# First feed-forward product in Strassen's form: 7 block products of 384 columns per pair of strips in place of 8

## The chip, the core and the metric

The kernel runs on one core of one Trainium2 chip. The metric is the device time of one execution in microseconds; beside each timed run stands one profiled execution with its trace. TensorE (PE in the profile) does the matmuls and loads their weights (PEld); VectorE (DVE), ScalarE (ACT) and GpSimd (POOL) do the element-wise work; SyncE (SP) issues most transfers.

## The reference

Two layers are applied to 768 tokens: 512 of a prompt and 256 of a sample. Only the second line of a layer is changed:

```
x = x + W_o( g_att * P_att(DiffAttn(n)) + g_rec * P_rec(BiRGLRU(n)) ),  n = RMSNorm(x)
h2 = rmsnorm(x, norm2_g)
x = x + jnp.square(jax.nn.relu(h2 @ w_ff1)) @ w_ff2      # 1024 -> 4096 -> 1024
```

## The kernel before

Everything is kept transposed: channels on the 128 partitions, the 768 tokens along the free axis, in two groups g of 512 and 256 (`GROUPS`). A float32 value is held as a rounded part hi and a remainder lo. Each product is three matmuls into one PSUM bank: hi by hi, hi by lo, lo by hi (`mm3`, L251 to L253). `split` makes the two parts: hi by a copy on ACT (L197), lo by a subtraction on DVE (L200).

**Weights.** A transfer of 512 KB brings 128 x 1024 numbers into one of two buffers `raw`; they are split into `whi` and `wlo`, four buffers each (`prefetch`, L233). A plan lists the strips in the order of use, and preparation may run 8 strips ahead.

**End of the mixers.** `wo_part` (L867) adds the 8 strips of `W_o` to the residual `xt`. `prep` (L294, L295) multiplies `xt` by the gain of the norm and splits it into `n2h` and `n2l`. The norm's factor over the tokens, `rb`, is not applied there but to the hidden values after the first product. For it, `squares` squares the 8 tiles of a group on ACT (L307), sums them on DVE in a chain of 7 dependent additions (L311) and splits the sum into two tiles `s`. `stats` sums `s` over the partitions by two matmuls with ones per group (L335, L336; result `nps`), and ACT and DVE make `rb` of it (L283 to L288).

**Feed-forward part.** 8 chunks c of 512 hidden channels per layer. In each, the first product FF1 has 4 strips s by 2 groups by 8 tiles of the contraction by 3 matmuls: 192, of 512 or 256 columns. Each result becomes hidden values: DVE takes the positive part times `rb` (L909), ACT squares it (L910), and it is split into `hh` and `hl`. The second product FF2 has 192 matmuls too, over the 4 tiles of the chunk, and its results are added to `xt` (L924). After the last chunk of layer 1 they go to the output (L929). In the chunk c = 0 the statistics stand on PE behind the first two strips, which are 96 matmuls, and their hidden values wait for `rb`.

**Order.** PE's order is the order of the program text. On the other engines a scheduler sorts the instructions when the kernel is built; each engine then works through its list in order.

Of the kernel before, what the change touches and what calls it, by code (L numbers as in the profile page):

```python
# [72 lines left out]
def trunk_kernel(ctx: ExitStack, tc: tile.TileContext, xT, wqk, wv, wx, wy, wg0, wg1, wa, wr, wo, wf1, wf2,  # L73
# [32 lines left out]
    def small_params(l, ap_):  # L106
# [99 lines left out]
    for l in range(DEPTH):  # L206
# [172 lines left out]
    for l in range(DEPTH):  # L379
# [453 lines left out]
        for j in range(KT):  # L833
            if j >= NF:
                w1 = wload("wr", l, j)
            m = ep.tile([P, T], F32, tag="sg", name=nm("m"), bufs=2)
# [8 lines left out]
            if j < 4:  # L845
                hi = recp.tile([P, T], F32R, tag="r", name=nm("mh"))
                lo = recp.tile([P, T], F32R, tag="r", name=nm("ml"))
            else:
                hi, lo = slot(gl, F32R), slot(gl, F32R)
# [10 lines left out]
        wso = {}  # L860

        def wo_part(j, g):
            if j not in wso:
                wso[j] = wload("wo", l, j)
            off, n = GROUPS[g]
            ps = strip(ppf, wso[j], (mh, ml), g)
            V.tensor_tensor(out=xt[j][:, off:off + n], in0=xt[j][:, off:off + n], in1=ps, op=ALU.add)  # L867

        LAG = 0
        for j in range(KT + LAG):  # L870
            if j < KT:
                wo_part(j, 0)
            if j >= LAG:
                wo_part(j - LAG, 1)


        n2h = [ep.tile([P, T], F32R, tag="e", name=nm("n2h")) for k in range(KT)]
# [7 lines left out]
        for c in range(NC_):  # L885
# [129 lines left out]
```

## Time and profile before

| | us |
|---|---|
| median of 3 runs (lowest, highest) | 2740.41 (2739.55, 2741.24) |
| the profiled execution | 2740.3 |
| its span | 2738.5 |
| PE busy | 2706.5 (99%) |
| DVE busy | 1639.8 (60%) |
| ACT busy | 1321.9 (48%) |

The feed-forward part of layer 0 runs from 838.9 to about 1373 us of the span, that of layer 1 from about 2201 to 2735. Matmuls overlap in the pipeline, so their durations add up to more than the time; what one costs is read from the distance between two starts.

### The profile page before, as it was taken

How to read it: one execution, taken by the hardware profiler on the slowest of the kernel's cores; microseconds unless marked ns; L12 is line 12 of the kernel's file. 1: busy time of each engine (PE TensorE's matmuls, PEld its weight loads, DVE VectorE, ACT ScalarE, POOL GpSimd, SP SyncE). 2: the span in 40 equal slices, each digit the busy share in tenths (PEclk: the TensorE clock that was granted, in tenths of full speed). 3: DMA queues.
4: the chain of work that ended last, by engine and by line, in shares of the span. 5: the costliest groups of instructions: out<-in, count | busy, mean ns of one | idle time of the engine just before them, and what ended most of it. 6: DMA issues, size and time to landing. Idle time of an engine off the chain costs nothing.

```text
span 2738.5 us, 41111 instructions
## 1 busy us (share of the span) xinstructions
PE 2706.5 (99%) x16840; PEld 2437.8 (89%) x16840; DVE 1639.8 (60%) x2970; ACT 1321.9 (48%) x2293; POOL 96.1 (4%) x134
## 2 busy tenths in 40 slices
PE   8999999999999999999999999999999999999999
PEld 8999888888888888888899998888888888888888
DVE  8878873797545443444578878637984454444443
ACT  7777871568324222222367878616773242222221
POOL 0000000000110000000000000000002100000000
PEclk9999999999999999999999999999999999999999
DMA  3111123121321112111221111231223211121111
GB/s 130 58 44 62 42 101 109 55 70 66 132 92 62 62 64 68 62 62 62 99 74 45 57 47 51 97 108 53 72 70 139 85 62 62 62 69 63 62 62 70
DMA packets 57485, 199.36 MB, mean 73 GB/s; under 512 B 7504, under 2 KB 9936, under 8 KB 57296
## 3 DMA queue, kind: packets, MB, share of 16 engines
q1 hardware_dynamic: 48384, 161.50, 17.8%
q0 software_dynamic: 8192, 34.61, 3.5%
q8 instruction: 132, 2.16, 0.3%
q10 hardware_dynamic: 720, 0.62, 0.1%
q14 instruction: 57, 0.47, 0.1%
HBM read 177.83 MB, written 18.87 MB: 72 GB/s over the span
## 4 chain that ended last, share of the span: by engine, by line
PE 86%; DVE 7%; ACT 5%; issue 1%; DMA 0%; ACTq 0%; DVEq 0%
PE d L251 19%; PE d L252 19%; PE d L253 19%; PE d L399 4%; PE d L398 4%; PE d L397 4%; PE s L574 3%; PE d L276 2%; PE d L275 2%; PE d L277 2%; PE d L526 1%; PE d L524 1%; PE d L525 1%; DVE t L808 1%; PE t L597 1%
## 5 line engine op out<-in xcount | busy, mean ns | idle before, releaser
L197 ACT ACTIVATE whi<-raw 128x1024 fp32r<-128x1024 f32 (+1 forms) x304 | 315.0, 1037 | 771.1 <-PE d L252 627.7
L200 DVE TENSOR_TENSOR wlo<-raw,whi 128x1024 fp32r<-128x1024 f32 (+1 forms) x304 | 369.5, 1217 | 120.5 <-ACT whi L197 119.0
L252 PE MATMUL d<-n2l,whi 128*128 128x512 f32 (+1 forms) x1024 | 344.8, 337 | 0.0
L251 PE MATMUL d<-n2h,whi 128*128 128x512 f32 (+1 forms) x1024 | 344.5, 336 | 0.0
L253 PE MATMUL d<-n2h,wlo 128*128 128x512 f32 (+1 forms) x1024 | 344.1, 336 | 0.0
L252 PE MATMUL d<-sX,whi 128*128 128x512 f32 (+1 forms) x704 | 237.0, 337 | 0.0
L251 PE MATMUL d<-sY,whi 128*128 128x512 f32 (+1 forms) x640 | 215.4, 337 | 0.3 <-DVE rec L344 0.3
L253 PE MATMUL d<-sY,wlo 128*128 128x512 f32 (+1 forms) x640 | 215.1, 336 | 0.0
L251 PEld LDWEIGHTS d<-n2h,whi 128*128 128x128 f32 x1024 | 194.4, 190 | 20.8
L253 PEld LDWEIGHTS d<-n2h,wlo 128*128 128x128 f32 x1024 | 194.2, 190 | 20.5
L252 PEld LDWEIGHTS d<-n2l,whi 128*128 128x128 f32 x1024 | 194.4, 190 | 20.0
L910 ACT ACTIVATE fr<-fr 128x512 f32<-128x512 f32 (+1 forms) x128 | 65.9, 515 | 270.6 <-DVE fr L909 270.6
L909 DVE SCALAR_TENSOR_TENSOR fr<-d,rb 128x512 f32<-128x512 f32 (+1 forms) x128 | 71.4, 558 | 176.5 <-PE d L253 168.9
L252 PE MATMUL d<-hl,whi 128*128 128x256 f32 (+1 forms) x512 | 172.4, 337 | 0.0
L251 PE MATMUL d<-hh,whi 128*128 128x256 f32 (+1 forms) x512 | 172.3, 336 | 0.0
L253 PE MATMUL d<-hh,wlo 128*128 128x256 f32 (+1 forms) x512 | 172.0, 336 | 0.0
L924 DVE TENSOR_TENSOR sZ<-sZ,d 128x256 f32<-128x256 f32 (+1 forms) x128 | 71.0, 554 | 141.6 <-PE d L253 141.6
L251 PE MATMUL d<-sZ,whi 128*128 128x512 f32 (+1 forms) x448 | 150.8, 337 | 0.3 <-DVE rec L344 0.3
L252 PE MATMUL d<-sZ,whi 128*128 128x512 f32 (+1 forms) x448 | 150.8, 336 | 0.0
L253 PE MATMUL d<-sZ,wlo 128*128 128x512 f32 (+1 forms) x448 | 150.6, 336 | 0.0
L397 PE MATMUL d<-whi,sY 128*128 128x256 f32 x512 | 147.8, 289 | 0.0
L397 PE MATMUL d<-whi,sZ 128*128 128x256 f32 x512 | 147.8, 289 | 0.0
(311 smaller groups left out, 7373.0 us busy)
## 6 DMA issues: line engine op xcount, KB each, us to landing
raw<-wf SPq DMA_DIRECT2D x128, 512.0 KB, 3.2
raw<-wqk SPq DMA_DIRECT2D x32, 512.0 KB, 3.3
raw<-wg SPq DMA_DIRECT2D x32, 512.0 KB, 3.3
raw<-wv SPq DMA_DIRECT2D x16, 512.0 KB, 3.8
raw<-wa SPq DMA_DIRECT2D x16, 512.0 KB, 4.2
raw<-wx SPq DMA_DIRECT2D x16, 512.0 KB, 3.3
raw<-wy SPq DMA_DIRECT2D x16, 512.0 KB, 3.2
raw<-wr SPq DMA_DIRECT2D x16, 512.0 KB, 3.4
```

What stands on the lines that cost most here:

```text
L197: S.activation(hi, src, AF.Copy)
L200: V.tensor_tensor(out=lo, in0=src, in1=hi.bitcast(F32), op=ALU.subtract)
L251: PE.matmul(ps, lhsT=wh, rhs=xh, start=(k == 0), stop=False)
L252: PE.matmul(ps, lhsT=wh, rhs=xl, start=False, stop=False)
L253: PE.matmul(ps, lhsT=wl, rhs=xh, start=False, stop=(k == n - 1))
L397: PE.matmul(j, lhsT=xh, rhs=hi[:, kk], start=(k == 0), stop=False)
L398: PE.matmul(j, lhsT=xh, rhs=lo[:, kk], start=False, stop=False)
L399: PE.matmul(j, lhsT=xl, rhs=hi[:, kk], start=False, stop=(k == 7))
L574: PE.matmul(pss[c], lhsT=z["q"][:, c, qs], rhs=kk[:, c, off:off + n], start=(x == 0), stop=(x == 1))
L909: V.scalar_tensor_tensor(out=r_, in0=ps, scalar=0.0, in1=rb2[:, off:off + n], op0=ALU.max, op1=ALU.mult)
L910: S.activation(r_, r_, AF.Square, scale=0.5)
L924: V.tensor_tensor(out=xg, in0=xg, in1=ps, op=ALU.add)
```

## The change

The tokens are cut into two halves of 384 (`TS`), the contraction of FF1 into two halves of 4 tiles, and the strips of a chunk into two pairs p. For each pair the 2 x 2 x 2 = 8 block products become 7 (`FP` lists all 14 of a chunk as p and product number), each of 4 tiles by 3 matmuls of 384 columns. That is 168 matmuls per chunk in place of 192.

**Operands of the tokens.** The 7 operands are scaled values or sums of blocks of `xt`, with the gain applied and split: products 1 and 5 from `ff_prep1` while the first four strips of `W_o` run, 6, 7 and 4 from `ff_prep2` in the next four, 2 and 3 behind them. They replace `prep`.

**Operands of the weights.** Four transfers bring a1, b1, b2, a2 (a1 and b1 into two new buffers `rw`); four DVE additions of 128 x 1024 make P1, P2, P3 and P4 of them, and the 7 operands a1, P1, P2, a2, P3, b2, P4 are each split. So a chunk has 11 splits of weights in place of 8, with the 4 of FF2.

**Results.** A PSUM bank takes several products where Strassen's form only adds them; otherwise ACT copies the bank out (L987, L989, L994) and DVE adds or subtracts (L991, L995, L1000): 6 copies and 6 additions per chunk. `hidden` is called 8 times per chunk, on 384 columns. FF2 keeps 192 matmuls, now all of 384 columns, with 16 additions to `xt` (L1015).

**Statistics.** In the chunk c = 0 they stand behind 6 of the 14 products, which are 72 matmuls.

```diff
...
+TH = T // 2
+TS = (slice(0, TH), slice(TH, T))
...
+FW = ("a1", "P1", "P2", "a2", "P3", "b2", "P4")
+FP = ((0, 1), (1, 1), (0, 5), (1, 5), (0, 6), (1, 6), (0, 2), (0, 7), (1, 2), (1, 7), (0, 4), (0, 3), (1, 4), (1, 3))
...
-            plan += [("wf1", l, c * 4 + s) for s in range(4)] + [("wf2", l, c * 4 + s) for s in range(4)]
+            plan += [("wf1", l, c, x) for x in FW] + [("wf2", l, c * 4 + s) for s in range(4)]
     pos = [0]
+    fw, fpool = {}, [None]
+    def ff_operand(l, c, x):
+        ep_ = fpool[0]
+        if x == "a1":
+            for i, y in enumerate(("a1", "b1", "b2", "a2")):
+                if i < 2:
+                    fw[y] = ep_.tile([P, 1024], F32, tag="rw", name=nm("rw"), bufs=2)
+                else:
+                    fw[y] = wp.tile([P, 1024], F32, tag="raw", name=nm("raw"), bufs=2)
+                nc.sync.dma_start(out=fw[y], in_=wf1[l][c][i])
+        elif x in ("P1", "P2"):
+            u, v = ("b1", "b2") if x == "P1" else ("P1", "a1")
+            fw[x] = ep_.tile([P, 1024], F32, tag="ws", name=nm("ws"), bufs=2)
+            V.tensor_tensor(out=fw[x], in0=fw[u], in1=fw[v], op=ALU.add)
+        elif x == "P3":
+            fw[x] = fw["b1"]
+            V.tensor_tensor(out=fw[x], in0=fw["a1"], in1=fw["b1"], op=ALU.add)
+        elif x == "P4":
+            fw[x] = fw["P2"]
+            V.tensor_tensor(out=fw[x], in0=fw["P2"], in1=fw["a2"], op=ALU.add)
+        return fw[x]
...
+        def halves(o, k):
+            ops[o][k] = t_ = slot(gx, F32R) if o in (1, 5) else rslot(F32R) if o in (2, 3) else eslot(F32R)
+            return t_[:, 0:TH], t_[:, TH:T]
+        def split2(o, k, src, gain=None):
+            hi, lo = halves(o, k)
+            if gain is None:
+                split(hi, lo, src)
+            else:
+                S.activation(hi, src, AF.Copy, scale=gain)
+                V.scalar_tensor_tensor(out=lo, in0=src, scalar=gain, in1=hi.bitcast(F32), op0=ALU.mult, op1=ALU.subtract)
+        gn = lambda k: v_[:, V_N2 + k:V_N2 + k + 1]
+        diff = [eslot() for i in range(2)]
+        def ff_prep1(k):
+            x, d = xt[k], diff[k // 2][:, TS[k % 2]]
+            split2(1, k, x[:, TS[0]], prm["ng2"][:, k:k + 1])
+            V.tensor_tensor(out=d, in0=x[:, TS[0]], in1=x[:, TS[1]], op=ALU.subtract)
+            split2(5, k, d, gn(k))
+        def ff_prep2(k):
+            x, x2, d = xt[k], xt[k + 4], diff[k // 2][:, TS[k % 2]]
+            t_ = eslot()
+            u, w = (t_[:, t] for t in TS)
+            S.activation(u, x2[:, TS[1]], AF.Copy, scale=gn(k + 4))
+            V.scalar_tensor_tensor(out=w, in0=d, scalar=gn(k), in1=u, op0=ALU.mult, op1=ALU.add)
+            split2(6, k, w)
+            V.scalar_tensor_tensor(out=u, in0=x[:, TS[1]], scalar=gn(k), in1=u, op0=ALU.mult, op1=ALU.subtract)
+            split2(7, k, u)
+            V.scalar_tensor_tensor(out=w, in0=x2[:, TS[0]], scalar=gn(k + 4), in1=w, op0=ALU.mult, op1=ALU.subtract)
+            split2(4, k, w)
+        for j in range(KT):
+            w1 = wload("wo", l, j)
+            for g in range(2):
+                off, n = GROUPS[g]
+                ps = strip(ppf, w1, (mh, ml), g)
+                V.tensor_tensor(out=xt[j][:, off:off + n], in0=xt[j][:, off:off + n], in1=ps, op=ALU.add)
+            if j < 4:
+                ff_prep1(j)
+            else:
+                ff_prep2(j - 4)
+        for o in (2, 3):
+            for k in range(4):
+                split2(o, k, xt[k + 4][:, TS[o - 2]], gn(k + 4))
...
+            def hidden(s, t, z, r_):
+                for i in range(2):
+                    if (s, i) not in hs:
+                        hs[s, i] = slot(gl, F32R) if not last else eslot(F32R) if s < 2 else rslot(F32R)
+                hi, lo = (hs[s, i][:, TS[t]] for i in range(2))
+                V.scalar_tensor_tensor(out=r_, in0=z, scalar=0.0, in1=rb2[:, TS[t]], op0=ALU.max, op1=ALU.mult)
+                S.activation(r_, r_, AF.Square, scale=0.5)
+                split(hi, lo, r_)
...
+            for i, (p, q) in enumerate(FP):
+                x, b = {1: ("a1", 2), 5: ("P1", 3), 6: ("P2", 2), 2: ("a2", 1), 7: ("P3", 2), 4: ("b2", 2), 3: ("P4", 3)}[q]
+                if x not in ws:
+                    ws[x] = [a.rearrange("p (h k c) -> p h k c", h=2, c=P)[:, :] for a in wload("wf1", l, c, x)]
+                hi, lo = (a[:, p] for a in ws[x])
+                new = q in (1, 5, 2)
+                if new:
+                    bank[p, b] = ppf.tile([P, TH], F32, tag="d", name=nm("d"))
+                ps = bank[p, b]
+                for k in range(4):
+                    oh, ol = (ops[q][k][:, t] for t in TS)
+                    PE.matmul(ps, lhsT=hi[:, k], rhs=oh, start=new and k == 0, stop=False, skip_group_check=True)
+                    PE.matmul(ps, lhsT=hi[:, k], rhs=ol, start=False, stop=False, skip_group_check=True)
+                    PE.matmul(ps, lhsT=lo[:, k], rhs=oh, start=False, stop=k == 3, skip_group_check=True)
+                m1, m16, u3, y4 = (z[:, TS[p]] for z in zz)
+                if q == 1:
+                    S.activation(m1, ps, AF.Copy, scale=-1.0)
+                elif q == 6:
+                    S.activation(m16, ps, AF.Copy, scale=-1.0)
+                elif q == 2:
+                    V.tensor_tensor(out=m1, in0=m1, in1=ps, op=ALU.add)
+                    hidden(2 * p, 0, m1, m1)
+                elif q == 7:
+                    S.activation(u3, ps, AF.Copy)
+                    V.tensor_tensor(out=u3, in0=u3, in1=bank[p, 3], op=ALU.subtract)
+                    hidden(2 * p + 1, 1, u3, u3)
+                elif q == 4:
+                    hidden(2 * p + 1, 0, ps, y4)
+                elif q == 3:
+                    V.tensor_tensor(out=m16, in0=m16, in1=ps, op=ALU.add)
+                    hidden(2 * p, 1, m16, m16)
+                if c == 0 and i == 5:
                     for g_ in range(2):
                         stats(nss[g_], rb2, None, g_, lambda n, s: mp.tile([P, n], F32, tag=gl, name=nm(s)), ppf, "d")
...
+            for s in range(4):
+                hi, lo = (a.rearrange("p (j k c) -> p j k c", j=2, c=P) for a in wload("wf2", l, c * 4 + s))
+                for t in range(2):
+                    for jj in range(2):
+                        j = 2 * s + jj
+                        ps = ppf.tile([P, TH], F32, tag="d", name=nm("d"))
+                        mm3(ps, [(hi[:, jj, k], lo[:, jj, k], hs[k, 0][:, TS[t]], hs[k, 1][:, TS[t]])
+                                 for k in ((0, 1, 2, 3), (0, 1, 3, 2))[t]])
+                        xg = xt[j][:, TS[t]]
+                        V.tensor_tensor(out=xg, in0=xg, in1=ps, op=ALU.add)
...
```

On PE, at the statistics of layer 0 (`nps` the sums; `s` the split sums of squares, first of 512 tokens, then of 256), before:

```order
L253 MATMUL d_1642_9398<-n2h_1595_9207,wlo_1555_8797 128x256
L335 MATMUL nps_1643_9423<-s_1613_9272,ones_71 128x512
L336 MATMUL nps_1643_9423<-s_1614_9273,ones_71 128x512
L335 MATMUL nps_1646_9434<-s_1623_9299,ones_71 128x256
L336 MATMUL nps_1646_9434<-s_1624_9300,ones_71 128x256
L251 MATMUL d_1656_9470<-n2h_1588_9200,whi_1559_8854 128x512
```

and now (lines of the changed kernel; `e`, `r` are operands of the tokens):

```order
L984 MATMUL d_1650_9391<-e_1610_9277,wlo_1569_8879 128x384
L370 MATMUL nps_1659_9469<-s_1630_9336,ones_71 128x512
L371 MATMUL nps_1659_9469<-s_1631_9337,ones_71 128x512
L370 MATMUL nps_1662_9480<-s_1640_9363,ones_71 128x256
L371 MATMUL nps_1662_9480<-s_1641_9364,ones_71 128x256
L982 MATMUL d_1671_9502<-r_1613_9288,whi_1574_8941 128x384
```

The statistics still stand in one block, now behind the sixth product. On DVE, where the sums of squares `sq` are made in layer 0, before:

```order
L867 TENSOR_TENSOR sY_1547_8734<-sY_1547_8734,d_1587_9174 128x256
L311 TENSOR_TENSOR sq_1605_9249<-sq_1605_9249,sq_1607_9254 128x512
L200 TENSOR_TENSOR wlo_1565_8913<-raw_1563_8910,whi_1564_8912 128x1024
L295 SCALAR_TENSOR_TENSOR n2l_1603_9215<-sY_1547_8734,vec0_78,n2h_1595_9207 128x256
L311 TENSOR_TENSOR sq_1605_9249<-sq_1605_9249,sq_1608_9257 128x512
...
L200 TENSOR_TENSOR s_1614_9273<-sq_1605_9249,s_1613_9272 128x512
...
L200 TENSOR_TENSOR wlo_1570_8971<-raw_1568_8968,whi_1569_8970 128x1024
...
L200 TENSOR_TENSOR s_1624_9300<-sq_1615_9276,s_1623_9299 128x256
L200 TENSOR_TENSOR wlo_1575_9029<-raw_1573_9026,whi_1574_9028 128x1024
```

and now, from the last addition of `W_o` (L941) on:

```order
L941 TENSOR_TENSOR sY_1547_8736<-sY_1547_8736,d_1608_9248 128x256
...
L209 TENSOR_TENSOR wlo_1581_9006<-rw_1551_8742,whi_1580_9005 128x1024
...
L346 TENSOR_TENSOR sq_1622_9313<-sq_1622_9313,sq_1623_9315 128x512
L346 TENSOR_TENSOR sq_1622_9313<-sq_1622_9313,sq_1624_9318 128x512
L209 TENSOR_TENSOR wlo_1589_9076<-raw_1552_8744,whi_1588_9075 128x1024
L346 TENSOR_TENSOR sq_1622_9313<-sq_1622_9313,sq_1625_9321 128x512
...
L209 TENSOR_TENSOR s_1631_9337<-sq_1622_9313,s_1630_9336 128x512
L209 TENSOR_TENSOR wlo_1597_9147<-ws_1567_8876,whi_1596_9146 128x1024
L346 TENSOR_TENSOR sq_1632_9340<-sq_1632_9340,sq_1633_9342 128x256
...
L209 TENSOR_TENSOR s_1641_9364<-sq_1632_9340,s_1640_9363 128x256
```

Before, one of the 7 additions of the first group (L311) stands ahead of the last addition of `W_o`. Now all 14 stand behind it, and behind 13 other instructions first: 11 of 384 columns and two splits of weights. The split of b2 (`wlo_1589`) stands between the second and the third addition, that of P4 (`wlo_1597`) ahead of the whole second group. The order in layer 1 is the same. On DVE, at the join of FF1 and FF2 in the third chunk of layer 0, before:

```order
L909 SCALAR_TENSOR_TENSOR fr_1730_10111<-d_1729_10086,rb_1604_9216 128x256
L200 TENSOR_TENSOR wlo_1690_9785<-raw_1688_9782,whi_1689_9784 128x1024
L200 TENSOR_TENSOR hl_1702_9851<-fr_1730_10111,hh_1701_9850 128x256
L924 TENSOR_TENSOR sY_1540_8720<-sY_1540_8720,d_1734_10122 128x512
L924 TENSOR_TENSOR sY_1541_8722<-sY_1541_8722,d_1735_10136 128x512
```

and now (`sZ` holds the hidden values; `rw` and `raw` are b1 and b2 of the next chunk, `ws` its P1):

```order
L209 TENSOR_TENSOR sZ_1815_10623<-e_1783_10431,sZ_1814_10622 128x384
L1000 TENSOR_TENSOR e_1781_10429<-e_1781_10429,d_1793_10485 128x384
L209 TENSOR_TENSOR wlo_1796_10501<-raw_1794_10498,whi_1795_10500 128x1024
L964 SCALAR_TENSOR_TENSOR e_1781_10429<-e_1781_10429,rb_1621_9312 128x384
L1015 TENSOR_TENSOR sY_1540_8722<-sY_1540_8722,d_1823_10709 128x384
L248 TENSOR_TENSOR ws_1806_10562<-rw_1798_10532,raw_1799_10534 128x1024
L209 TENSOR_TENSOR sZ_1813_10603<-e_1781_10429,sZ_1812_10602 128x384
```

Ahead of the last remainder of the hidden values there now stands an addition for the next chunk's weights, which needs the transfer of that chunk's b2.

## Rows read from the trace of the kernel before

**Rows 1.** The page: busy time by engine, and the chain by engine

```profile
PE 2706.5 (99%) x16840; PEld 2437.8 (89%) x16840; DVE 1639.8 (60%) x2970; ACT 1321.9 (48%) x2293; POOL 96.1 (4%) x134
...
PE 86%; DVE 7%; ACT 5%; issue 1%; DMA 0%; ACTq 0%; DVEq 0%
```

**Rows 2.** Waits of PE: line, waited for: us in total, times, longest us

```profile
PE t L546 <- DVE q L554: 8.2, 10, 1.8
PE d L475 <- ACT sY L294: 7.3, 1, 7.3
```

**Rows 3.** Windows, a chunk each: length; busy us by engine; clock, DMA share, GB/s

```profile
839.00:906.00 67.00, 67.00 (x387) 59.24 (x386) 37.76 (x61) 26.25 (x48) 0.00 (x0) 1.00 0.19 63
...
1039.00:1106.00 67.00, 67.00 (x388) 59.34 (x388) 27.25 (x40) 16.45 (x24) 0.00 (x0) 1.00 0.19 63
```

**Rows 4.** Timeline of PE in FF2 and at its end: start us, us, instruction

```profile
1099.77 0.39 PE L252 MATMUL d<-hl,whi 128*128 128x512 f32 x1
...
1103.39 0.39 PE L253 MATMUL d<-hh,wlo 128*128 128x512 f32 x1
1103.62 0.28 PE L251 MATMUL d<-hh,whi 128*128 128x256 f32 x1
...
1106.49 0.40 PE L251 MATMUL d<-n2h,whi 128*128 128x512 f32 x1
```

**Rows 5.** Timeline of PE around the statistics of layer 0

```profile
838.91 0.40 PE L251 MATMUL d<-n2h,whi 128*128 128x512 f32 x1
...
855.59 0.39 PE L335 MATMUL nps<-s,ones 128*128 128x512 f32 x1
...
856.29 0.39 PE L251 MATMUL d<-n2h,whi 128*128 128x512 f32 x1
```

**Rows 6.** Timeline of DVE there (x5: five in a row)

```profile
842.17 3.87 DVE L311 TENSOR_TENSOR sq<-sq,sq 128x512 f32<-128x512 f32 x5
846.74 0.69 DVE L200 TENSOR_TENSOR s<-sq,s 128x512 fp32r<-128x512 f32 x1 [0.70 <-ACT s L197]
...
848.92 1.23 DVE L200 TENSOR_TENSOR wlo<-raw,whi 128x1024 fp32r<-128x1024 f32 x1
850.06 2.01 DVE L311 TENSOR_TENSOR sq<-sq,sq 128x256 f32<-128x256 f32 x4
852.55 0.42 DVE L200 TENSOR_TENSOR s<-sq,s 128x256 fp32r<-128x256 f32 x1 [0.48 <-ACT s L197]
```

**Rows 7.** Timeline of ACT there

```profile
846.07 0.63 ACT L197 ACTIVATE s<-sq 128x512 fp32r<-128x512 f32 x1 [2.53 <-DVE sq L311]
...
847.84 1.05 ACT L197 ACTIVATE whi<-raw 128x1024 fp32r<-128x1024 f32 x1
848.79 1.32 ACT L307 ACTIVATE sq<-sY 128x256 f32<-128x256 f32 x4
```

**Rows 8.** Groups on DVE by form, 1039 to 1106: busy us, mean ns, idle

```profile
L200 DVE TENSOR_TENSOR wlo<-raw,whi 128x1024 fp32r<-128x1024 f32 x8 | 9.8, 1226 | 4.4 <-ACT whi L197 4.4
L924 DVE TENSOR_TENSOR sY<-sY,d 128x512 f32<-128x512 f32 x8 | 5.5, 687 | 10.0 <-PE d L253 10.0
L924 DVE TENSOR_TENSOR sY<-sY,d 128x256 f32<-128x256 f32 x8 | 3.4, 421 | 7.1 <-PE d L253 7.1
```

**Rows 9.** Groups on ACT by form, 1039 to 1106

```profile
L910 ACT ACTIVATE fr<-fr 128x512 f32<-128x512 f32 x4 | 2.5, 632 | 18.7 <-DVE fr L909 18.7
```

**Rows 10.** Timeline of PE at the start of the span

```profile
9.80 0.42 PE L475 MATMUL d<-whi,sY 128*128 128x256 f32 x1
...
12.57 0.39 PE L476 MATMUL d<-wlo,sY 128*128 128x256 f32 x1
12.79 0.30 PE L477 MATMUL d<-whi,sZ 128*128 128x256 f32 x1
```

**Rows 11.** Transfers from 906 to 972: KB each, median us from issue to landing

```profile
raw<-wf SPq DMA_DIRECT2D x8, 512.0 KB, 3.3
```

**Rows 12.** Timeline of DVE at the end of the span

```profile
2735.28 0.42 DVE L924 TENSOR_TENSOR sZ<-sZ,d 128x256 f32<-128x256 f32 x1 [1.02 <-PE d L253]
```

More of the change, by code (lines that the diff above doesn't have):

```diff
@@ L844, in trunk_kernel @@
             G.tensor_tensor(out=m, in0=m, in1=sg, op=ALU.add)
[L845 to L849, printed above, removed]
+            hi, lo = (rslot(F32R) if j < 4 else slot(gl, F32R) for i in range(2))
             split(hi, lo, m)
@@ L859, in trunk_kernel @@
             xt.append(t_)
[L860 to L874, printed above, removed]
@@ L877, in trunk_kernel @@
[L877 to L878 removed]
+        ops = {o: [None] * 4 for o in range(1, 8)}
+        def halves(o, k):
[8 more added lines that the diff above has]
+                V.scalar_tensor_tensor(out=lo, in0=src, scalar=gain, in1=hi.bitcast(F32), op0=ALU.mult, op1=ALU.subtract)
@@ L885, in trunk_kernel @@
         for c in range(NC_):
-            hh, hl, ws = [], [], {}
-            for s in range(4):
-                if c % 2 == 1:
-                    hh.append(recp.tile([P, T], F32R, tag="r", name=nm("hh")))
-                    hl.append(recp.tile([P, T], F32R, tag="r", name=nm("hl")))
-                else:
-                    hh.append(slot(gx, F32R))
-                    hl.append(slot(gx, F32R))
-            order = [(s, g) for s in range(4) for g in range(2)]
-            wait = []
-            for s, g in order:
-                if s not in ws:
-                    ws[s] = wload("wf1", l, c * 4 + s)
-                wait.append((s, g, strip(ppf, ws[s], (n2h, n2l), g)))
-                if c == 0 and s < 2:
-                    if (s, g) != (1, 1):
-                        continue
+            last = c == NC_ - 1
@@ new lines, in trunk_kernel @@
+            ws, bank = {}, {}
+            zz = [eslot() for i in range(4)]
+            for i, (p, q) in enumerate(FP):
[30 more added lines that the diff above has]
+                if c == 0 and i == 5:
@@ L904, in trunk_kernel @@
                     for g_ in range(2):
                         stats(nss[g_], rb2, None, g_, lambda n, s: mp.tile([P, n], F32, tag=gl, name=nm(s)), ppf, "d")
-                for s_, g_, ps in wait:
-                    off, n = GROUPS[g_]
-                    r_ = ep.tile([P, n], F32, tag="sg", name=nm("fr"), bufs=2)
-                    V.scalar_tensor_tensor(out=r_, in0=ps, scalar=0.0, in1=rb2[:, off:off + n], op0=ALU.max, op1=ALU.mult)
-                    S.activation(r_, r_, AF.Square, scale=0.5)
-                    split(hh[s_][:, off:off + n], hl[s_][:, off:off + n], r_)
@@ L912, in trunk_kernel @@
[L912 to L929 removed]
+            for s in range(4):
[8 more added lines that the diff above has]
+                        V.tensor_tensor(out=xg, in0=xg, in1=ps, op=ALU.add)
+                        if last:
+                            if l + 1 < DEPTH:
+                                G.dma_start(out=xs[j][:, TS[t]], in_=xg)
+                            else:
+                                nc.sync.dma_start(out=out[j][:, TS[t]], in_=xg)
```

57 lines of the change are left out of this document (23 added, 34 removed).

## The prediction

> **What bounds the kernel now.** I read the page first. PE is busy for 2706.5 of 2738.5 us, and 86% of the chain of work that ended last is PE's [rows 1]. The waits of PE come next: the largest single one is 7.3 us at the start of the span, the largest sum 8.2 us in ten pieces in attention, and none is named in the feed-forward part [rows 2]. In the windows of one chunk each PE is busy for all of 67 us at a clock of 1.00, DVE for 37.76 us in the chunk with the statistics and 27.25 us in an ordinary one, ACT for 26.25 and 16.45 [rows 3]. So this part lasts as long as its matmuls, and a matmul less is time gained, unless another engine takes that away. For what one matmul takes I read the timeline, from start to start: 16 steps from 1099.77 to 1103.39 give 0.226 us for 512 columns, 24 steps from 1103.62 to 1106.49 give 0.120 us for 256 [rows 4].
>
> **What is gained.** No matmul of 384 columns stands in the feed-forward part of before. The two sizes bound it, 0.120 and 0.226; I take the middle, 0.173 us, since a cost that grows evenly with the columns lies there. A product of 12 matmuls takes 2.08 us. FF1 of a chunk was 96 x (0.226 + 0.120) = 33.2 us and becomes 168 x 0.173 = 29.1; FF2 keeps its columns: 192 x 0.173 = 33.2. The gain is 24 x 0.173 = 4.15 us per chunk, 66.4 us in 16 chunks. At the ends of the bound the 360 matmuls would take 43 or 81 us in place of the 66.4 of before, 370 us gained or 240 lost in 16 chunks; a cost that stays at either end over a change of 128 columns is unlikely, and rival 4 keeps it.
>
> The row says 0.226 and 0.120. The Trainium skill (TensorE: Matmul & The Clock Gate, "Back-to-back issue gap") gives the columns over 2.4 GHz plus about 2.5 ns, which is 0.216, 0.109 and, at 384, 0.1625 us. Both sizes in the trace are 10 ns longer, so the trace disagrees with the rule by a constant, and the row decides; by the rule the gain would be 62.4 us.
>
> **What is added and hidden.** Costs at 384 columns are taken half way between the rows of 512 and 256: 0.55 us on DVE (0.687 and 0.421) [rows 8], about 0.5 on ACT (0.632 at 512) [rows 9]. When such instructions stand in a row the next starts some 0.08 earlier (848.92 to 850.06 is 1.14 for an instruction of 1.23) [rows 6], so 0.475 and 0.44 in a queue. Per chunk, DVE has 11 splits and 4 additions of 128 x 1024 at 1.226 [rows 8] (18.4 us), 16 additions of FF2, 6 of combinations and 8 x 2 of hidden values at 0.55 (20.9): 39 of 62.3 us. ACT has 11 splits at 1.05 [rows 7] and 6 copies, 8 squares and 8 roundings at 0.5: 23 us. Both have room on average, so what they cost is decided where PE waits for a particular result. The transfers stay the same in bytes; one lands 3.3 us after issue [rows 11], and a weight now serves 4.2 us of PE in FF1 where it served 8.3, with four buffers ahead of it; counting the releases through a chunk leaves 7 us or more to each operand.
>
> **Term 1, the statistics of c = 0.** Before, FF1 starts at 838.91, and PE reaches the statistics at 855.59, 16.7 us later; the last split sum of squares was ready at 852.55 + 0.42 = 852.97, 14.1 us after the start, so nothing waited [rows 5, 6]. Now PE reaches them after 6 x 2.08 = 12.5 us. That alone would leave PE waiting for 14.1 - 12.5 = 1.6 us, plus some 0.2 to be told. But the sums also come later, because DVE works its list in order. From the start of FF1:
> - the last addition of `W_o` starts at 0.2 and takes 0.34 in the queue; then come 11 short instructions (5.2) and two splits of weights (2.3): 8.0.
> - The first two of the 7 additions depend on each other: five such took 3.87, so 0.774 each [rows 6]: 9.6.
> - Then the split of b2. ACT rounds it behind the operands' and six of the eight squares, 7.6 us of its own work plus waits for DVE's sums, at about 9.4 to 10.4, so DVE's half ends at 11.5. The five additions left end at 15.4, ACT's rounding of the sum (0.63) at 16.1 [rows 7], the remainder (0.69) at 16.8 [rows 6].
> - ACT now rounds P4 (to 17.1), DVE splits it (to 18.2), and only then come the seven additions of 256 columns at 2.01 / 4 = 0.503 [rows 6]: 21.8. The two halves of the split, 0.42 each, end at 22.7; PE goes on at 22.9.
>
> PE does the first group's statistics meanwhile, 0.46 of the 0.70 us that the block takes (855.59 to 856.29) [rows 5], so it loses about 22.9 - 12.5 - 0.6 = 9.8 us per layer, **19.6 us** in the two. Bounds: without the splits of b2 and P4 in the way (1.9 and 2.1 us) and with everything a little earlier, 5 us a layer; with 0.1 more at each of some twenty steps that wait for one another, 12. I take the value of the count.
>
> **Term 2, the clock after that wait.** At the start of the span PE had waited for 7.3 us [rows 2]; the matmuls of 256 columns then start 0.213 us apart from 9.80 to 12.57 and 0.12 apart later [rows 4, 10], 1.2 GHz in place of 2.4, which costs 14 x 0.093 = 1.3 us. A wait of 9.8 us is longer, so I take 1.35 us a layer, **2.7 us**; the bounds are 0 and 1.4 a layer. The Trainium skill (TensorE: Matmul & The Clock Gate, "HAM oscillation — how this bites in real kernels") says that a TensorE left idle falls back to half its clock and must earn it again; this speaks against a change that brings a wait where none was, and the start of this span agrees (14 matmuls at half speed).
>
> **Term 3, the join of FF1 and FF2.** The last hidden values need a copy, an addition, `hidden` and a split behind the last product. FF2 starts 29.1 us into a chunk and takes, within a strip, the unready tiles last. The half t = 0 of strip 3 comes at about 30.4 and is wanted at 30.9. The half t = 1 of strip 2 stands on DVE behind the addition for the next P1, which needs the next b2: its buffer comes free at about 29.9 (the split of FF2's third strip, whose own buffers the product 13 releases at 27.0), it lands 3.3 us later [rows 11] at 33.2, the addition takes 1.15, the remainder 0.5: 34.9. It is wanted at 29.1 + 2 x 2.08 + 9 x 0.173 + a matmul = 35.0. So the margin is 0.1 us, and below it nothing is gained. I take 0.2 us in each of 14 chunks, **3 us**; bounds 0 and 1 us a chunk (0 to 14 us).
>
> **Term 4, the end.** The last addition has 384 columns where it had 256 (0.42 us [rows 12]), and the last transfer half as much again: **0.3 us**. The operands of the tokens are made while `W_o` runs; the last ones are wanted 8.3 us into FF1 (product 6) and are ready by about 5, so they cost nothing but Term 1's delay.
>
> **The sum.** 2740.3 (profiled; the median is 0.1 above it) - 66.4 + 19.6 + 2.7 + 3.0 + 0.3 = 2699.5, so **2699 us**. A difference of 0.2%, 5.5 us, is about what a measurement can tell.
>
> **Rivals.**
> 1. The statistics are nearly covered: the sums follow the scheduler's list faster than I count, and PE loses 2 to 5 us a layer, at full clock. 2740.3 - 66.4 + 0.3 + 4 to 10, with joins of 0 to 5: 2678 to 2689. For it: before, the same sums took 14.1 us with splits between them [rows 6]. Against it: two splits of weights, 11 short instructions and a late start now stand ahead.
> 2. The joins wait: landing or DVE later by half a microsecond or more than in Term 3. At 1 us a chunk in 14 chunks the sum is 2699 + 11 = 2710; range 2708 to 2722. For it: a margin of 0.1 us. Against it: the median landing varies little.
> 3. Slower than before: DVE's list. The addition for P1 waits at the join for a transfer, and everything behind it waits too. It turns the sign when each of 16 chunks loses more than (2740.3 - 2696.5) / 16 = 2.7 us, that is when b2 lands some 6.1 us after issue in place of 3.3 [rows 11]; at 7 us it costs 3.6 x 16 and gives about 2755.
> 4. The change does not do what it says, since 384 columns do not cost the middle: as much as 512, they make both products slower and the time about 2740 + 16 x (360 x 0.226 - 66.4) + 25 = 3004. By the gap that the Trainium skill gives (the same section), the 360 matmuls of a chunk would take 58.5 us in place of 62.3, and the time would be about 2638; both sizes in [rows 4] speak against it.
>
> **How the numbers follow.** The forecast with its bounds (stalls of 8 to 11.5 us, clock 0 to 1.4, joins 0 to 0.6) spans 2690 to 2708 and has 0.66. Rival 1 has 0.12, rival 2 0.13, rival 3 0.04, rival 4 0.03 (0.01 of it fast), something near no change 0.02. The range 2682 to 2715 cuts off a quarter of rival 1 and a third of rival 2 and all of 3 and 4: about 0.16. Faster: 0.66 + 0.12 + 0.13 + 0.01 = 0.92; same 0.02; slower 0.06.
>
> **What would show it.** In the profile of the changed kernel: starts of matmuls of 384 columns 0.173 us apart; a chunk of some 62.3 us; a wait of PE for `s` of the second group of about 6 us after one of 4 for the first, twice; a stretch of half clock behind each; waits of PE on hidden values at the joins of no more than a few tenths. The prediction is wrong if PE passes the statistics with less than 5 us lost, if the joins lose over 0.6 us each, or if waits for `whi` or `wlo` stand in FF1.

## The result

| | before | changed |
|---|---|---|
| median (lowest, highest), us | 2740.39 (2739.55, 2741.24) | 2695.95 (2695.55, 2698.56) |
| the profiled execution, its span, us | 2740.3, 2738.5 | 2696.0, 2694.2 |
| PE busy, us | 2706.5 (99%) | 2645.3 (98%) |
| DVE busy, us | 1639.8 (60%) | 1832.7 (68%) |
| ACT busy, us | 1321.9 (48%) | 1414.6 (53%) |

The changed kernel takes 0.984 of the time, with an interval of 0.9823 to 0.9857: faster by 44 us, where 2699, 41 us less, was forecast. By the spans the difference is 44.3 us, and it lies in the two feed-forward parts: 21.2 us in layer 0, 23.1 in layer 1; the mixers of layer 1 between them take 827.3 us in both kernels.

The changed kernel's page and its waits of PE answer to [rows 1, 2]:

```profile
PE 2645.3 (98%) x16456; PEld 2496.6 (93%) x16456; DVE 1832.7 (68%) x3236; ACT 1414.6 (53%) x2469; POOL 95.3 (4%) x134
...
PE 84%; DVE 8%; ACT 6%; issue 2%; DMA 0%; ACTq 0%; DVEq 0%
```

```profile
PE nps L370 <- ACT s L206: 10.7, 2, 5.7
PE t L581 <- DVE q L589: 8.3, 10, 1.8
PE d L510 <- ACT sY L329: 7.6, 1, 7.6
PE d L982 <- ACT e L987: 5.4, 2, 2.7
```

Two waits are new, each twice: that of the statistics for `s`, and one of a product (L982) for a copy of ACT (L987). The windows, a chunk each, answer to [rows 3]:

```profile
838.50:913.80 75.30, 66.88 (x360) 65.94 (x359) 54.10 (x86) 35.45 (x65) 0.00 (x0) 0.93 0.17 57
1038.50:1100.90 62.40, 62.40 (x362) 62.40 (x361) 37.34 (x53) 21.29 (x33) 0.00 (x0) 1.00 0.21 68
```

An ordinary chunk is full of matmuls at a clock of 1.00, with 37.3 us of DVE's work where I had worked out 39. In the chunk with the statistics PE is busy for 66.9 of 75.3 us, and the mean granted clock falls to 0.93. The timeline of PE in that chunk of layer 0, from the end of the fourth product on, and below it that of layer 1, tell how it comes about:

```profile
846.67 0.34 PE L984 MATMUL d<-sX,wlo 128*128 128x384 f32 x1
849.71 0.44 PE L982 MATMUL d<-e,whi 128*128 128x384 f32 x1 [2.70 <-ACT e L987]
...
853.31 0.52 PE L983 MATMUL d<-e,whi 128*128 128x384 f32 x1
853.63 0.52 PE L984 MATMUL d<-e,wlo 128*128 128x384 f32 x1
...
855.81 0.40 PE L371 MATMUL nps<-s,ones 128*128 128x512 f32 x1
861.93 0.58 PE L370 MATMUL nps<-s,ones 128*128 128x256 f32 x1 [5.72 <-ACT s L206]
862.39 0.58 PE L371 MATMUL nps<-s,ones 128*128 128x256 f32 x1
862.77 0.53 PE L982 MATMUL d<-r,whi 128*128 128x384 f32 x1
```

```profile
2190.24 0.45 PE L982 MATMUL d<-e,whi 128*128 128x384 f32 x1 [2.71 <-ACT e L987]
...
2195.47 0.50 PE L371 MATMUL nps<-s,ones 128*128 128x512 f32 x1 [0.23 <-DVE s L209]
2200.91 0.58 PE L370 MATMUL nps<-s,ones 128*128 128x256 f32 x1 [4.93 <-ACT s L206]
```

In layer 0 PE waits ahead of the fifth product, runs a stretch of the fifth and sixth at half speed (853.31 to 853.63 is 0.32 us where 0.173 is usual), reaches the statistics of the first group without a wait, waits again for the sum of the second group, and runs at half speed once more. Layer 1 has the same two waits, but no half clock behind the first. The lists of DVE and ACT around it answer to [rows 6, 7]. DVE, then ACT:

```profile
847.30 1.41 DVE L346 TENSOR_TENSOR sq<-sq,sq 128x512 f32<-128x512 f32 x2
848.64 1.22 DVE L209 TENSOR_TENSOR wlo<-raw,whi 128x1024 fp32r<-128x1024 f32 x1
849.77 3.73 DVE L346 TENSOR_TENSOR sq<-sq,sq 128x512 f32<-128x512 f32 x5
854.33 0.69 DVE L209 TENSOR_TENSOR s<-sq,s 128x512 fp32r<-128x512 f32 x1 [0.83 <-ACT s L206]
856.69 1.23 DVE L209 TENSOR_TENSOR wlo<-ws,whi 128x1024 fp32r<-128x1024 f32 x1 [1.67 <-ACT whi L206]
857.83 3.59 DVE L346 TENSOR_TENSOR sq<-sq,sq 128x256 f32<-128x256 f32 x7
861.91 0.43 DVE L209 TENSOR_TENSOR s<-sq,s 128x256 fp32r<-128x256 f32 x1 [0.48 <-ACT s L206]
```

```profile
847.21 1.04 ACT L206 ACTIVATE whi<-raw 128x1024 fp32r<-128x1024 f32 x1
848.15 1.13 ACT L342 ACTIVATE sq<-sY 128x512 f32<-128x512 f32 x2
849.19 0.84 ACT L987 ACTIVATE e<-d 128x384 f32<-128x384 f32 x2
...
855.60 1.06 ACT L206 ACTIVATE whi<-ws 128x1024 fp32r<-128x1024 f32 x1 [1.30 <-PE d L983]
856.56 2.54 ACT L342 ACTIVATE sq<-sY 128x256 f32<-128x256 f32 x8
```

The second wait is the one forecast. The first is not: product 6 of the first pair adds to the bank of product 1, whose negated content ACT has to copy first. That copy (849.19) stands behind two squares and the rounding of b2 (847.21). The rounding followed other squares without a pause. It could not have begun much earlier either: its buffer comes free with the products that use P1, and their last matmul with the rounded part starts at 846.50 and takes 0.33 us.

### The profile page after: what moved, and what is told of

Same layout as the page of the kernel before. It is cut to its first block, busy times and chain, and to the rows that moved or that the text cites. A ratio compares the mean times of both kernels' runs of the same rounds, so it can differ in the third digit from the quotient of the medians.

```text
span 2694.2 us, 40709 instructions
## 1 busy us (share of the span) xinstructions
PE 2645.3 (98%) x16456; PEld 2496.6 (93%) x16456; DVE 1832.7 (68%) x3236; ACT 1414.6 (53%) x2469; POOL 95.3 (4%) x134
## 4 chain that ended last, share of the span: by engine, by line
PE 84%; DVE 8%; ACT 6%; issue 2%; DMA 0%; ACTq 0%; DVEq 0%
PE d L286 13%; PE d L288 13%; PE d L287 13%; PE d L982 6%; PE d L983 6%; PE d L984 6%; PE d L433 4%; PE d L434 4%; PE d L432 4%; PE s L609 3%; PE d L311 2%; PE d L310 2%; PE d L312 2%; PE d L561 2%; PE d L559 2%
## 5 line engine op out<-in xcount | busy, mean ns | idle before, releaser
L286 PE MATMUL d<-sZ,whi 128*128 128x384 f32 (+2 forms) x896 | 300.4, 335 | 0.3 <-DVE rec L379 0.3
L287 PE MATMUL d<-sX,whi 128*128 128x384 f32 (+2 forms) x896 | 300.5, 335 | 0.0
L287 PE MATMUL d<-sZ,whi 128*128 128x384 f32 (+2 forms) x896 | 300.4, 335 | 0.0
L288 PE MATMUL d<-sZ,wlo 128*128 128x384 f32 (+2 forms) x896 | 300.2, 335 | 0.0
L286 PEld LDWEIGHTS d<-sZ,whi 128*128 128x128 f32 x896 | 169.1, 189 | 9.4 <-DVE rec L379 0.5
L288 PEld LDWEIGHTS d<-sZ,wlo 128*128 128x128 f32 x896 | 169.1, 189 | 9.0
L287 PEld LDWEIGHTS d<-sX,whi 128*128 128x128 f32 x896 | 169.1, 189 | 9.0
L287 PEld LDWEIGHTS d<-sZ,whi 128*128 128x128 f32 x896 | 169.1, 189 | 8.8
L286 PE MATMUL d<-sX,whi 128*128 128x384 f32 (+2 forms) x512 | 171.1, 334 | 0.0
L288 PE MATMUL d<-sX,wlo 128*128 128x384 f32 (+2 forms) x512 | 171.1, 334 | 0.0
L432 PE MATMUL d<-whi,sZ 128*128 128x256 f32 x512 | 148.1, 289 | 0.0
L197 ACT ACTIVATE p<-s,nb,sc 128x512 f32<-128x512 f32 (+1 forms) x192 | 134.6, 703 | 21.2 <-DVE nb L612 19.5
L434 PE MATMUL d<-whi,sX 128*128 128x256 f32 x512 | 145.3, 284 | 0.0
L433 PE MATMUL d<-wlo,sZ 128*128 128x256 f32 x512 | 145.2, 284 | 0.0
L434 PE MATMUL d<-whi,sZ 128*128 128x256 f32 x512 | 144.8, 283 | 0.0
L1015 DVE TENSOR_TENSOR sZ<-sZ,d 128x384 f32<-128x384 f32 x128 | 69.6, 553 | 109.2 <-PE d L288 109.2
L982 PE MATMUL d<-e,whi 128*128 128x384 f32 x384 | 129.4, 337 | 5.4 <-ACT e L987 5.4
```

What stands on the lines that cost most here:

```text
L197: return used(S.activation(*a, **k))
L286: PE.matmul(ps, lhsT=wh, rhs=xh, start=(k == 0), stop=False)
L287: PE.matmul(ps, lhsT=wh, rhs=xl, start=False, stop=False)
L288: PE.matmul(ps, lhsT=wl, rhs=xh, start=False, stop=(k == n - 1))
L432: PE.matmul(j, lhsT=xh, rhs=hi[:, kk], start=(k == 0), stop=False)
L433: PE.matmul(j, lhsT=xh, rhs=lo[:, kk], start=False, stop=False)
```

## The experiments

Losses of the chunk c = 0 are counted here against 62.40 us per chunk (the distance between the starts of FF2 in two chunks, 1068.87 and 1131.27) and 0.70 us for the statistics: 513.24 us from the first matmul of the part to the next layer's give 13.3 us in layer 0, and 511.4 us, to the end of the last matmul's step, give 11.5 in layer 1. The expectations below counted with 62.35 and name 13.7 and 11.9.

**The sums of squares made while `W_o` runs.** The squares go through the still unused tile of `rb` into two PSUM banks, tile by tile:

```diff
+                sq = rb2[:, off:off + n] if j else acc[g]
+                S.activation(sq, xt[j][:, off:off + n], AF.Square)
+                if j:
+                    V.tensor_tensor(out=acc[g], in0=acc[g], in1=sq, op=ALU.add)
...
-        nss = [squares(xt, g, lambda n, dt, s: mp.tile([P, n], dt, tag=gl, name=nm(s))) for g in range(2)]
```

> The squares of each residual tile are made and added up right behind its W_o strip, in two PSUM banks, in place of all behind the last strip. My theory: the 13.7 and 11.9 us that the chunk c = 0 loses in the two layers come from the sums of squares standing in DVE's list behind the operands and two splits of weights, and from ACT's list, where the rounding of b2 waits for product 3 and holds the copy that product 4 needs. Then the wait of PE for s goes (5.7 and 4.9 us, with the half clock behind it, some 2.8 us each), while a wait for the copy of about 2 us stays with its half clock: a loss of about 4 us a layer, about 2678 us. Rival: DVE has too much work in the 24 us around the start of FF1, whatever its order; then the wait only changes its name, to whi, wlo or an operand, and the time stays at 2690 to 2696. A second rival: the added work in the W_o stage makes PE wait there, and the gain is smaller by that.

Measured: 2675.9 us (0.9767 of before, 0.9753 to 0.9782). The timeline of PE:

```profile
847.18 0.34 PE L993 MATMUL d<-sX,wlo 128*128 128x384 f32 x1
849.28 0.45 PE L991 MATMUL d<-e,whi 128*128 128x384 f32 x1 [1.76 <-ACT e L996]
...
853.58 0.39 PE L370 MATMUL nps<-s,ones 128*128 128x512 f32 x1
853.81 0.39 PE L371 MATMUL nps<-s,ones 128*128 128x512 f32 x1
854.04 0.28 PE L370 MATMUL nps<-s,ones 128*128 128x256 f32 x1
```

No wait for `s` is left, and no half clock; the wait for the copy stays, 1.8 us in place of 2.7, now behind the rounding of b2 and that of one operand of the tokens. The loss falls to 2.1 and 3.2 us. The added work stands beside `W_o` at no cost: in the 66.5 us ahead of FF1 PE has no gap, and DVE is busy for 47.4 us there, where it was for 42.3 in the changed kernel.

```profile
772.00:838.50 66.50, 66.50 (x384) 58.83 (x384) 47.35 (x73) 27.82 (x46) 1.85 (x1) 1.00 0.14 48
```

So the place of the squares and their sums in the lists was the cause, not the amount of work. The edit moves the squares on ACT together with the sums on DVE; which of the two lists alone would have been enough is not shown.

**The same, and a2's products ahead of P2's in c = 0.**

```diff
+FW0 = ("a1", "P1", "a2", "P2", "P3", "b2", "P4")
...
+FP0 = ((0, 1), (1, 1), (0, 5), (1, 5), (0, 2), (1, 2), (0, 6), (1, 6), (0, 7), (1, 7), (0, 4), (0, 3), (1, 4), (1, 3))
...
```

The hidden values of the two products with a2 now stand behind the statistics, since they need `rb`.

> As e1, and in c = 0 alone the products run in another order: the two with a2, which start a new bank, stand ahead of the two with P2, which add to a bank that ACT has to copy first. My theory: the wait for the copy goes too, because PE comes to that bank 4.2 us later and the rounding of b2 is then done. c = 0 loses 0 to 1 us a layer: 2670 to 2672. Rival: the copy is late for another reason (its place behind the operands), and the wait only moves by two products: 2676 to 2679.

Measured: 2674.5 us (0.9761, 0.9745 to 0.9777), 2.5 us above what I expected; the losses are 0.8 and 2.0 us. The wait ahead of the first P2 product is gone. What is left in c = 0 is half a microsecond a layer at the tenth product, on a copy again, and in both e1 and e2 some tenths at joins of layer 1 (the remainder of a hidden tile, 0.8 and 0.6 us). It is the fastest version here; the step from e1 to e2, 1.4 us, is less than its runs differ among themselves (2672.5 to 2674.9).

**The order of products alone, the sums left late.** The edit is that of the order of products and weights just above, on the changed kernel.

> The changed kernel with the order of products of e2 in c = 0 (those with a2 ahead of those with P2), and the sums of squares left where the changed kernel has them. PE no longer comes early to the bank that ACT must copy. My theory: the wait for the copy and the half clock behind it go, but the lists of DVE and ACT set when the second group's sum is there. In layer 0 the half clock had also delayed the release of P2's buffers and with it the rounding of P4, so the statistics of the second group start 21.9 us behind the start of FF1 (give or take 0.5) in both layers, where they started 23.4 and 21.9 behind it. Total -1 to -2 us, 2694 to 2695. Rival: the waits add up, and 2.9 us a layer and the half clock are gained in full: 2688 to 2689.

Measured: 2694.1 us (0.9833, 0.9817 to 0.9849). The wait for the copy is gone, and PE waits longer for `s` instead, now for the first group too (5.2 us, then 3.2 for the second, in each layer):

```profile
PE nps L374 <- ACT s L210: 16.9, 4, 5.2
```

The statistics of the second group start 22.6 us after FF1 in both layers, 0.2 later than the upper end of what I expected. In the profiled executions the feed-forward parts lose 13.1 and 12.2 us, where the changed kernel's lose 13.3 and 11.5. So the two waits of the changed kernel do not add up: without the wait for the copy, the waits for `s` are longer.

**The copy of product 1 on DVE in c = 0.**

```diff
...
+                        V.tensor_scalar(out=m1, in0=ps, scalar1=-1.0, scalar2=0.0, op0=ALU.mult, op1=ALU.add)
...
```

> In c = 0 the copy of product 1 (with its sign changed) is made by DVE in place of ACT; nothing else is changed. My theory: the first wait of PE (2.7 us) shrinks to about 1.6, since the copy no longer stands behind the rounding of b2 on ACT. But the statistics hang on DVE's list alone, which gets two copies longer, so PE goes on behind the statistics at about the same time as before (23.4 us after the start of FF1, within 0.7): the two waits are not added, the first is paid out of the second. Total change 0 to -2 us. Rival: the waits add up, and each us taken from the first is gained: -1.3 us a layer or more with the half clock behind it, so -3 to -6 us in all.

Measured in a single execution: 2693.4 us, 2.6 less than the changed kernel and so between the theory and the rival. The first wait is 1.60 us in both layers, as expected, and no half clock follows. Layer 1 gains 0.3 us, layer 0 2.1, more than the 0.7 that I allowed. In layer 0 of the changed kernel the half clock had delayed the sixth product, with it the buffers of P2, and so the rounding of P4 (1.30 us of ACT's idle time, released by PE, in the rows of ACT above), behind which the second group's seven additions stand. In layer 1 it had not: there the clock stayed at full speed. The other runs with the sums left late and the products in the old order agree: the second group's statistics start 23.2 to 23.4 us after FF1 where the half clock stands behind the first wait (layer 0 of the changed kernel, both layers in e4 and e6), and 21.9 in the changed kernel's layer 1, where it does not; in e7, with less work on DVE, they start at 22.7 in layer 0 with it and at 21.3 in layer 1 without.

**TensorE kept busy in the second wait.** The list `fill` has 40 entries for the second group of c = 0 and is empty elsewhere.

```diff
+        for f_ in fill:
+            PE.matmul(ps, lhsT=ones, rhs=f_, start=True, stop=True)
```

> 40 matmuls of 256 columns with ones (a result that is overwritten) stand on PE ahead of the statistics of the second group, 4.8 us inside the wait for s of 5.7 and 4.9 us. They keep TensorE busy while it waits. My theory: the half clock behind that wait (16 matmuls 0.32 us apart in place of 0.173, and 0.6 us at the statistics) goes, the wait itself is as long as before: -2.8 us a layer, 2690 us. Rival: the half clock costs nothing, because the hidden values behind it wait for rb anyway: 2696.

Measured: 2692.1 us (0.9827, 0.9812 to 0.9841), 3.8 less than the changed kernel. The timeline of PE:

```profile
855.69 4.71 PE L371 MATMUL nps<-sX,ones 128*128 128x256 f32 x40
861.58 0.39 PE L372 MATMUL nps<-s,ones 128*128 128x256 f32 x1 [1.18 <-ACT s L206]
862.04 0.39 PE L373 MATMUL nps<-s,ones 128*128 128x256 f32 x1
862.26 0.34 PE L984 MATMUL d<-r,whi 128*128 128x384 f32 x1
862.44 0.34 PE L985 MATMUL d<-r,whi 128*128 128x384 f32 x1
```

The statistics start 23.4 us after FF1 in both layers, and the matmuls behind them run at full speed. In layer 0 that is the start that the changed kernel had, and the layer gains 2.3 us. Layer 1 gains only 0.2: in this run the half clock came behind its first wait as well, where the changed kernel's profiled run had none, and the statistics start 1.5 us later than there. So the half clock has a price of its own, about 2.3 us behind a wait of 5.7 us. Rival and theory lie 5.6 us apart here and the measurement between them, nearer to the theory.

**The tokens in halves without Strassen's form.** FF1 and FF2 of the kernel before on 384 and 384 columns:

```diff
...
+        HALF = ((0, T // 2), (T // 2, T // 2))
...
-                off, n = GROUPS[g]
+                off, n = HALF[g]
...
```

> The kernel before with the tokens of the feed-forward part cut into halves of 384 in place of 512 and 256, and nothing of Strassen's form: 8 products per pair of strips. My theory: the columns cost evenly, and only the first matmuls of each block of 512, 0.232 us apart in place of 0.226, are saved: 384 x 0.1733 = 66.5 us per chunk in place of 66.7, -3 us in 16 chunks, 2737 us; the 7 products in place of 8 are then worth 24 x 0.1733 x 16 = 66.5. Rival: the 3.4 us that the matmuls gained beyond my 66.4 come from elsewhere (waits at the joins of before), and this kernel takes as long as before: 2740.

Measured: 2737.2 us (0.9991, 0.9982 to 1.0001), 2.2 us below the kernel before in the same series and at the expected value. The interval still holds no difference at all, so the times alone do not settle it; the traces do. The first matmul of a chunk follows that of the chunk before it in 66.56 us:

```profile
1105.69 0.33 PE L251 MATMUL d<-n2h,whi 128*128 128x384 f32 x1
...
1172.25 0.33 PE L251 MATMUL d<-n2h,whi 128*128 128x384 f32 x1
```

In the kernel before, 1106.49 [rows 4] to this row, it is 66.72:

```profile
1173.21 0.40 PE L251 MATMUL d<-n2h,whi 128*128 128x512 f32 x1
```

So 384 columns cost what lies between 512 and 256 in a kernel without Strassen's form too, and 0.16 of the 4.32 us that a chunk gained is the cut into halves.

**The hidden tiles of FF2 in plain order.**

```diff
-                                 for k in ((0, 1, 2, 3), (0, 1, 3, 2))[t]])
+                                 for k in ((0, 1, 2, 3), (0, 1, 2, 3))[t]])
```

> The changed kernel, but FF2's products of the second half of the tokens take the hidden tiles in the order 0, 1, 2, 3 in place of 0, 1, 3, 2, so that PE wants the last remainder 3 x 0.173 = 0.52 us earlier. In the trace of the changed kernel it is ready 0.35 us ahead of its matmul. My theory: PE now waits for 0.17 us, with the telling some 0.2 to 0.35, at each of 14 joins: +3 to +5 us, 2699 to 2701. By the margin of 0.1 us in my prediction it would be 0.42 x 14 = +6 us, 2702. Rival: DVE's list shifts and gives the time back, 2696.

Measured: 2701.6 us (0.9858, 0.9844 to 0.9873), 5.6 more than the changed kernel. PE now steps 0.41 and 0.28 us around the matmul that needs the last remainder, where 0.173 is usual:

```profile
1074.85 0.34 PE L286 MATMUL d<-sZ,whi 128*128 128x384 f32 x1
1075.26 0.45 PE L287 MATMUL d<-sZ,whi 128*128 128x384 f32 x1
1075.54 0.34 PE L288 MATMUL d<-sZ,wlo 128*128 128x384 f32 x1
```

A chunk takes 62.7 us in place of 62.40 there, which is 4 to 5 us in 14 joins, as expected from a margin of 0.35 us; the rest of the 5.6 fits the half clock behind the first wait, which this run shows in both layers (8 matmuls in layer 1, about 1.2 us, where the changed kernel had none).

**No additions of weights** (b1, a1 and a2 stand in the products in place of their sums).

```diff
...
-            V.tensor_tensor(out=fw[x], in0=fw[u], in1=fw[v], op=ALU.add)
+            fw[x] = fw[u]
...
```

> The changed kernel without the four additions of weights per chunk: the products take b1, a1 and a2 themselves in the place of their sums, so the output is not the reference's. That takes 4 x 1.15 = 4.6 us of 37.3 per chunk from DVE. My theory: they are hidden, and PE's waits in the chunks 1 to 7 are none with or without them; the chunk c = 0 hangs on the sums of squares and changes by less than 1 us a layer: 2694 to 2697. Rival: the additions delay the splits or the last hidden values by some tenths in each chunk that the trace puts down to nothing: 16 x 0.2 to 0.4, so 2690 to 2693.

Measured: 2693.5 us (0.9832, 0.9817 to 0.9847), half a microsecond below what I expected and as far above the rival's range. DVE's busy time in an ordinary chunk falls from 37.34 to 32.98 us, and PE is as full as before. In the profiled runs the feed-forward parts are 0.4 and 0.3 us shorter, with waits in c = 0 of 2.5 and 5.2 us in place of 2.7 and 5.7. By the trace, then, the additions are hidden; the 2.5 us between the medians are not explained by a row, and the spans of the two profiled executions differ by 1.0.

**The statistics behind ten products.**

```diff
...
-                if c == 0 and i == 5:
+                if c == 0 and i == 9:
...
```

> The changed kernel with the statistics behind 10 products in place of 6, and the hidden values of the products 2 and 7 behind them. PE then comes to the statistics some 25 us after the start of FF1, behind the s of the second group (24 us). My theory: the wait for s goes, but rb comes about 8 us later in the list of products, and all 8 pieces of hidden values stand behind it, 1.2 us each on DVE: FF2's first product waits for four of them, 4 to 6 us, so c = 0 loses 9 to 12 us a layer in place of 13.7 and 11.9: 2690 to 2696. Rival: the hidden values are made in time and only the wait for the copy of product 1 with its half clock is left, 3 to 4.5 us a layer: 2676 to 2679.

Measured in a single execution: 2700.1 us, 4 above the upper end of the theory and 21 above the rival's. The waits of PE:

```profile
PE d L286 <- ACT sX L206: 6.2, 2, 4.2
PE d L286 <- ACT sZ L206: 5.8, 2, 3.8
PE d L982 <- ACT e L987: 5.4, 2, 2.7
```

No wait for `s` is left; FF2's first products wait for hidden values instead, about 6 us a layer, with half clock behind it. Layer 0 loses as much as in the changed kernel, layer 1 3.8 us more; in this run layer 1 has 17 matmuls at half clock behind the wait for the copy (about 2.5 us), which the changed kernel's layer 1 has not. Moving the statistics moves the wait; moving what they wait for (e1) removes it.

## Why the prediction was right

| term | forecast, us | measured, us |
|---|---|---|
| 24 matmuls less per chunk | -66.4 | -69.1 = 16 x (66.72 - 62.40) |
| c = 0, waits and clock (terms 1 and 2) | +22.3 | +24.8 = 13.3 + 11.5 |
| joins (term 3) | +3.0 | 0 |
| end and rest | +0.3 | 0.0 |
| sum | -40.8 | -44.3 |

The first three terms were off by 2.5 to 3 us each, in both directions. That the total came within 3.5 us of the measurement is partly luck.

**The gain** was right in its mechanism. The middle between the two rows gave 0.173 us per matmul, and the trace has 0.1733. What I undersized is the chunk of before: 0.226 was read in the middle of a block, and the first matmuls of each block of 512 columns stand 0.23 apart (1106.49 and 1106.72 in the kernel before), so its chunk takes 66.72 us and not 66.4. The rule weighed against the rows, columns over 2.4 GHz plus 2.5 ns (the Trainium skill, TensorE: Matmul & The Clock Gate, "Back-to-back issue gap"), would have been 0.1625; the trace disagrees at 384 as it did at 512 and 256. The same section gives that formula as the gap of an isolated matmul and says that a stream in which each matmul loads its weights departs from it, which the prediction left out.

**Term 1, the statistics**, was right in its main cause and about in size, and e1 shows the cause: take the squares and their sums out of the way, and about 20 us of the 24.8 go. The count by DVE's list put the second group's `s` at 22.7 us after the start of FF1; in layer 1 it was ready at 22.3 (2201.32), in layer 0 at 23.8. The 0.2 us that the count then allows until PE goes on stood on no row; e6 lost 0.34 us a join for a matmul wanted 0.17 us too early, which is of that size. But a step was missing: the fifth product waits for a copy on ACT, which the prediction did not have as an operation that a product waits for. It came to 2.9 us a layer, hid in the term because the time at which PE goes on hardly depends on it (e9, and layer 1 of e3), and moved PE's arrival at the first group's statistics behind its `s` in layer 0 and to 0.2 us ahead of its remainder in layer 1. So the wait of 4 us for the first group and 6 for the second, which I named as what the profile would show, came as 2.7 at the fifth product and 5.7 (4.9) at the second group. In layer 0 the missing step also made the end later by 1.1 us, over the half clock, the release of P2 and the rounding of P4.

**Term 2, the clock**, was forecast at 1.35 us a layer behind one wait. The waits themselves cost 17.6 us in the two layers (2.9 and 5.9 in layer 0; 2.9, 0.7 at the first group's statistics and 5.2 in layer 1) where term 1 had 19.6. The rest, 7.3 where term 2 had 2.7, is the clock and the first steps behind a wait: 4.6 us in layer 0, behind both waits, and 2.7 in layer 1. That an idle TensorE falls back to half its clock (the Trainium skill, TensorE: Matmul & The Clock Gate, "HAM oscillation — how this bites in real kernels") the trace shows in both layers: the granted clock is 0.50 from 862 to 865 us and from 2202 to 2205. I had taken the price of the start of the span, 14 matmuls of 256 columns; a matmul of 384 columns loses more at half speed (0.147 us in place of 0.093), and there was a second wait. So the two terms were off in opposite directions, and that their sum holds within 2.5 us is partly luck.

**Term 3, the joins**, was oversized: no wait of PE is named in the chunks 1 to 7, and their starts stand 62.40 us apart, once 62.51. The mechanism was right, and e6 shows it; the margin was 0.35 us and not 0.1. The rows of DVE at such a join in the changed kernel:

```profile
1071.88 0.55 DVE L1015 TENSOR_TENSOR sY<-sY,d 128x384 f32<-128x384 f32 x1
1072.72 1.23 DVE L248 TENSOR_TENSOR ws<-rw,raw 128x1024 f32<-128x1024 f32 x1 [0.30 <-DMA raw<-wf]
1073.86 0.55 DVE L209 TENSOR_TENSOR sZ<-e,sZ 128x384 fp32r<-128x384 f32 x1
```

The addition for P1 does wait for the transfer of b2, by 0.30 us, and holds the remainder behind it, which ends at 1074.41; the matmul that needs it starts at 1074.76:

```profile
1074.76 0.33 PE L287 MATMUL d<-sZ,whi 128*128 128x384 f32 x1
```

With so small a margin the honest value was a coin's toss between 0 and 3 us; the bounds held it.

**The rivals.** The statistics were not nearly covered, the joins did not wait, and DVE's list, although it sets the time in c = 0, did not set it elsewhere: 37.3 of 62.4 us, with additions whose removal changes a chunk by nothing (e7), although at the joins it was 0.35 us from doing so (e6). 384 columns cost the middle of 512 and 256.

## What to carry to other kernels

When a change takes work from the engine that bounds a kernel, the first place to look is where that engine is wanted by a result that does not get faster: here the statistics were due 4 us earlier on PE, and a chain of sums, which had had 2.6 us to spare and now stood further back in the lists, cost about 20 us in two layers (e1). Follow an in-order list instruction by instruction, and list for each product not only its operands but who must have read its bank. If a wait appears, move what is waited for and not the waiting: the sums made one stage earlier, where DVE had room, gave 20 us, the statistics moved later gave nothing (e8, one execution).

## What the runs showed of the hardware that was not expected

A wait of PE of 2.5 to 2.7 us can cost the clock. Ten such waits stand ahead of the fifth product (five kernels, two layers each; steps of 2.9 to 3.05 us between two matmuls). Seven of them brought 8 to 17 matmuls 0.32 us apart, the level of 1.2 GHz; three did not. In five of the seven the granted clock fell 0.9 to 1.3 us after PE had gone on. In the other two, layer 1 of e6 and of e8, it fell inside the wait, 0.3 and 0.7 us before its end, and the first matmul was slow already. The rows of e6:

```profile
2192.25 0.69 PE L982 MATMUL d<-e,whi 128*128 128x384 f32 x1 [2.70 <-ACT e L987]
2192.73 0.53 PE L983 MATMUL d<-e,whi 128*128 128x384 f32 x1
```

After the waits of 1.6 to 1.8 us at the same place (e1 and e3, four cases) PE ran at full clock up to its next wait. So a layer can take some 1.5 us more (10 matmuls at 0.147 us each) with nothing else changed, and a comparison of 1 to 3 us between such kernels has to be read layer by layer in the trace. Whether this is what sets the four times of the changed kernel apart, 2695.55 to 2698.56, is not shown: each kernel left one trace.
